# Loading the first feed-forward weights by rows of the contraction, zero matmuls ahead of them, one shared key block, and one filler moved

## The chip, the core and the metric

The kernel runs on one core of one Trainium2 chip. The metric is device time in microseconds (us) of one execution of the whole program. TensorE does the matmuls, ScalarE (ACT) and VectorE (DVE) the elementwise work, GpSimd (POOL) some of it, and SyncE (SP) issues most of the transfers from HBM.

## What is computed

The reference is two layers of an encoder for 320 tokens (256 of a prompt, 64 of a step with 256 cached ones), model width 1024. Cut to what matters here:

```python
for l in range(DEPTH):                                    # 2
    x = layer_norm(ALPHA * x + 0.5 * swiglu(x, f1_gu, f1_d), ...)      # 1024 -> 2 x 2816 -> 1024
    z = x @ w_in     # aq ak av  bq bk bv  iq ik iw  cq ck cv  gates
    bk = rope(bk, qpos)      # 64 columns: one key head for mixer B, returned too
    ik = rope(ik, qpos)      # 64 columns: one key head for B's indexer, returned too
    ...                      # mixers A (band), B (top-k by the indexer), C (differential), gated and merged
    x = layer_norm(ALPHA * x + merged @ w_out, ...)
    x = layer_norm(ALPHA * x + memory_attn(x, mem_k, mem_v, wm_q, wm_o), ...)
    x = layer_norm(ALPHA * x + 0.5 * swiglu(x, f2_gu, f2_d), ...)
```

The memory keys and values of the prompt (`mem_prompt @ w_mem_k`, `@ w_mem_v`) are computed for both layers as well.

## The kernel before, in words

Activations lie feature by token: a tile is 128 features by 320 tokens. Every fp32 value is kept as a pair, a rounded high part and the rest, so each product of a weight tile with an activation tile is three matmuls (`mm3`, L183 to L185: high by high, low by high, high by low). A weight block is 128 partitions by 1024 columns (512 KB); it holds the eight 128x128 tiles that one 128-wide output block contracts over. `prep` (L137 to L151) loads a block into a `raw` tile, ACT copies it to `hi` in two halves (L148) and DVE subtracts to get `lo` (L151). `raw`, `hi` and `lo` have three buffers each. `stream()` fixes the order of the blocks, and `ahead` and `nextw` keep two blocks ahead of the matmuls. A block is 24 matmuls of 320 columns.

The tile framework takes the program and decides the order on each engine by its own estimates; the queues are in order. Waits come from data, from buffers that are still read, and from PSUM: eight banks, four with the tag `mm` and four with the tag `at`.

**Start.** Before the first matmul the program loads one weight block in two halves and the input x (`load_x`, L202, and `split_x`, L205: cast, and subtraction on DVE and POOL). In the first feed-forward block (j = 0 of `ffn`, L485; L490 to L500) the gate product runs over all eight k's of x with the high part of the weights first, then with the low part; from then on every hidden block is a gate and an up product (48 matmuls in all) and an activation (L516 to L520).

**Mixers.** `attn_layer` (L531) projects values, then the index key `ik` and the four index queries (`QK0`), computes index scores and a top-k mask, and then runs the rest of the projections (`QK1`) in between the softmaxes of the three mixers. A mixer's turn is: scores (`scores`, L615, PE L625), softmax on DVE and ACT (`softmax`, L634 to L657), the transposition (`turn`, L660, PE L664 to L667), copies out of PSUM (for mixer C `c_turn`, L803, ACT L810 and DVE L811), the product with the values (`c_values`, L815, PE L817 to L822) with a root mean square on ACT (L828), POOL (L830, L831) and DVE (L834), and `c_finish` (L837). `projs(n)` (L848) puts n projections between these steps so that TensorE has work while the others finish. L667 writes a PSUM bank of the tag `at`, which the exponentials of the softmax last issued have to have read. `ik` and `bk` are both made by projecting the same 64 columns twice, so that the key lies on both halves of the partitions.

**Fillers.** The memory keys and values are 16 blocks for each layer, called fillers; they run inside the layer norms, where TensorE would wait. `FILL` (L62) says how many in each of the four norms of a layer. In a norm with n of them `before` (L1059, called after the fourth output block) runs n - 3, and `during` the last three while the statistics are formed. A filler's weights take a `raw` buffer too, and its `hi` and `lo` lie in tiles of the softmax.

Of the kernel before, what the change touches and what calls it, by code (L numbers as in the profile page):

```python
# [61 lines left out]
FILL = ((8, 8, 4, 4), (4, 4, 0, 0))  # L62
# [25 lines left out]
def ffn_stream(l, which):  # L88
    for j in range(FB):
# [8 lines left out]
def encoder(ctx: ExitStack, tc: tile.TileContext, a):  # L98
# [10 lines left out]
    def f(t):  # L109
        return t.bitcast(F32)  # L110
# [8 lines left out]
    def wtile(w=NT):  # L119
        return wk.tile([128, NT], F32, tag="w", bufs=8, name="w")[:, :w]  # L120
# [16 lines left out]
    def prep(src, cols, hi, lo, parts=1, hooks=None):  # L137
        raw = wp.tile([128, 1024], F32, tag="raw", name="raw")
        n = cols // parts
        for i in range(parts):  # L140
            c = slice(i * n, (i + 1) * n)
            if hooks:
                nc.sync.dma_start(raw[:, c], src[:, c])
            elif i == 0:
                nc.sync.dma_start(raw[:, :cols], src)
            if hooks:
                hooks[i][0]()
            act.activation(hi[:, c], raw[:, c], AF.Copy)  # L148
            if hooks:
                hooks[i][1]()  # L150
            dve.tensor_tensor(out=lo[:, c], in0=raw[:, c], in1=f(hi)[:, c], op=OP.subtract)  # L151
        return hi, lo
# [5 lines left out]
    def ahead(n, parts=2, hooks=None):  # L158
        while pos[0] < len(order) and len(ready) < n:
            key, cols = order[pos[0]]  # L160
            pos[0] += 1
            if key[0] == "wd":
                _, l, which, m, c0 = key
                src = a["wd"][l, which, m, :, c0 * 128:c0 * 128 + cols]
            else:
                src = a[key[0]]
                for i in key[1:]:
                    src = src[i]
            hi = wp.tile([128, 1024], F32R, tag="hi", name="hi")
            lo = wp.tile([128, 1024], F32R, tag="lo", name="lo")  # L170
            ready.append((key, prep(src, cols, hi, lo, parts, hooks)))
# [27 lines left out]
    x32 = one.tile([128, KB, NT], F32, name="x32")  # L199
# [11 lines left out]
    ahead(1, 2, ((lambda: (load_x(0), load_x(2)), lambda: split_x(0)),  # L211
                 (lambda: (load_x(4), load_x(6)), lambda: (split_x(2), split_x(4), split_x(6)))))
    ahead(2)
    x32 = [x32[:, m] for m in range(KB)]
# [269 lines left out]

    def ffn(l, which, x, norm):  # L485
        h = []
        for j in range(FB):
            pg, pu = psmm()[:, :NT], psmm()[:, :NT]
            wg = nextw("wgu", l, which, j, 0)
            if j == 0 and not (l or which):  # L490
                for k in range(KB):
                    c = slice(k * 128, (k + 1) * 128)
                    pe.matmul(pg, wg[0][:, c], x[k][0], start=(k == 0), stop=False)
                    pe.matmul(pg, wg[0][:, c], x[k][1], start=False, stop=False)
                for k in range(KB):
                    c = slice(k * 128, (k + 1) * 128)
                    pe.matmul(pg, wg[1][:, c], x[k][0], start=False, stop=(k == KB - 1))
                wu = nextw("wgu", l, which, j, 1)
                for k in range(KB):
                    mm3(pu, wu, x, k, k, k == 0, k == KB - 1)  # L500
            elif j == 0:
# [14 lines left out]
            s = wtile()  # L516
            act.activation(s, pg, AF.Silu)
            dve.tensor_tensor(out=s, in0=s, in1=pu, op=OP.mult)  # L518
            h.append(pair())
            split(s, h[j])  # L520
# [10 lines left out]
    def attn_layer(l, x, norm):  # L531
# [4 lines left out]
        kslot = {"ak": 0, "ck": 2, "bk": 6, "ik": 7}  # L536
        qk = {}
        SHUF = [(r + 8) % 16 if r < 16 else r for r in range(32)]

        def proj(name, i):  # L540
            p = block_mm(nextw("wqk", l, QK.index((name, i))), x)
# [12 lines left out]
            else:  # L554
                scaled = name in ("bq", "cq")
                sh, u = wtile(), wtile()
                dve.stream_shuffle(out=sh, in_=p, mask=SHUF)  # L557
                pool.tensor_tensor(out=sh, in0=sh, in1=sinS if scaled else sinT, op=OP.mult)  # L558
                dve.scalar_tensor_tensor(u, p, -0.125 if scaled else 1.0, cosT, op0=OP.mult, op1=OP.mult)
# [318 lines left out]
        projs(2)  # L878
# [347 lines left out]
```

## Time and profile before

| | |
|---|---|
| median of 3 runs | 1827.33 us (1826.3 to 1828.15) |
| the profiled execution: its own time | 1825.32 us |
| its span, first to last instruction | 1823.5 us |
| TensorE busy | 1770.3 us (97% of the span) |
| VectorE busy | 1158.6 us (64%) |
| ScalarE busy | 872.4 us (48%) |
| GpSimd busy | 274.1 us (15%) |
| mean granted TensorE clock | 0.991 of full speed |
| moved by DMA | 278.66 MB, 153 GB/s over the span |

The 1.8 us between the span and the execution's own time lie before the first and behind the last instruction. A row of the timeline gives the start in us from the span's start, the duration, engine and line of the kernel, operation, output and inputs by the program's names (without buffer numbers), partitions by columns, and in brackets how long the engine had been idle and whose end released it. A matmul's duration is longer than its distance to the next, since matmuls are pipelined: what one costs is read from the distance of two starts. "SPq" is a transfer being issued by SyncE. The granted clock is printed as a share of 2.4 GHz, so 0.5 is 1.2 GHz; up to the first record of a change, at 14.12 us, the view prints 1.00.

### The profile page before, as it was taken

Reading aid. Unit: us, or ns where it says so; the run is one execution under the profiler, and the core shown is the slowest. Engines: PE = TensorE matmul, PEld = TensorE weight load, DVE = VectorE, ACT = ScalarE, POOL = GpSimd, SP = SyncE. Lnnn points to the kernel's source line nnn. Section 1 sums busy time; section 2 is a strip of 40 time slices with the busy share of each in tenths; the row PEclk is TensorE's granted clock in tenths of the full one; section 3 lists DMA queues with packets and bytes.
Section 4 is the critical chain, followed back from the end, with each engine's and each line's share of the span. In section 5 each row is a group of like instructions: output and inputs, shape, how many; then the busy total and the mean of one; then the engine's idle time right before and its main releaser. Section 6 shows DMA issues by size and latency. Waiting matters only on the chain. (4 is left out here: it accounts for less than half of the span.)

```text
span 1823.5 us, 31668 instructions
## 1 busy us (share of the span) xinstructions
PE 1770.3 (97%) x12196; PEld 1718.2 (94%) x12196; DVE 1158.6 (64%) x2284; ACT 872.4 (48%) x1951; POOL 274.1 (15%) x297
## 2 busy tenths in 40 slices
PE   8999999989999999999999999999999999899997
PEld 8999999978998989999999999999889989899996
DVE  5544567986567785445564546679765786854455
ACT  5444435455455655444444444455554556444443
POOL 0000122230123040000210001222411220300012
PEclk9999999999999999999999999999999999999998
DMA  6544745434557544445544445454334572345442
GB/s 224 173 151 146 223 123 177 142 107 127 150 150 250 179 133 145 151 150 151 181 134 149 150 145 184 128 177 151 112 118 149 158 230 90 121 152 150 148 148 81
DMA packets 93176, 278.66 MB, mean 153 GB/s; under 512 B 12384, under 2 KB 26592, under 8 KB 92512
## 3 DMA queue, kind: packets, MB, share of 16 engines
q1 hardware_dynamic: 85536, 269.69, 48.1%
q10 hardware_dynamic: 7488, 6.95, 1.3%
q8 instruction: 95, 1.56, 0.3%
q14 instruction: 57, 0.47, 0.1%
HBM read 261.72 MB, written 14.88 MB: 152 GB/s over the span
## 5 line engine op out<-in xcount | busy, mean ns | idle before, releaser
L183 PE MATMUL mm<-slot,hi 128*128 128x320 f32 x3384 | 1054.5, 312 | 10.9 <-ACT slot L478 7.4
L185 PE MATMUL mm<-slot,hi 128*128 128x320 f32 x3384 | 1047.6, 310 | 1.7 <-DVE slot L480 1.6
L184 PE MATMUL mm<-slot,lo 128*128 128x320 f32 x3384 | 1048.5, 310 | 0.4 <-DVE lo L151 0.4
L151 DVE TENSOR_TENSOR lo<-raw,hi 128x512 fp32r<-128x512 f32 (+2 forms) x880 | 626.5, 750 | 362.3 <-ACT hi L148 359.4
L148 ACT ACTIVATE hi<-raw 128x512 fp32r<-128x512 f32 (+2 forms) x880 | 499.7, 614 | 579.8 <-issue 404.8
L183 PEld LDWEIGHTS mm<-slot,hi 128*128 128x128 f32 x3384 | 638.7, 189 | 18.9 <-ACT slot L478 8.9
L185 PEld LDWEIGHTS mm<-slot,hi 128*128 128x128 f32 x3384 | 637.4, 189 | 4.4 <-DVE slot L480 3.8
L184 PEld LDWEIGHTS mm<-slot,lo 128*128 128x128 f32 x3384 | 638.3, 189 | 1.1 <-DVE lo L151 0.8
L378 POOL TENSOR_TENSOR acc<-x 128x320 f32<-128x320 f32 x8 | 13.4, 1678 | 860.4 <-DVE x L407 681.8
L518 DVE TENSOR_TENSOR w<-w,mm 128x320 f32<-128x320 f32 x88 | 42.9, 488 | 132.1 <-PE mm L185 126.8
L378 POOL TENSOR_TENSOR acc<-acc,x 128x320 f32<-128x320 f32 x32 | 39.4, 1232 | 165.2 <-DVE x L407 165.2
L779 ACT ACTIVATE gate<-mm 128x320 f32<-128x320 f32 x48 | 21.0, 438 | 75.4 <-PE mm L185 75.4
L379 POOL TENSOR_TENSOR acc<-acc,w 128x320 f32<-128x320 f32 x40 | 49.9, 1247 | 39.6 <-ACT w L373 39.5
L558 POOL TENSOR_TENSOR w<-w,cst 128x320 f32<-128x320 f32 x32 | 28.1, 878 | 168.9 <-DVE w L557 119.2
L450 POOL TENSOR_TENSOR x<-x,msb 128x320 f32<-128x320 f32 x47 | 44.4, 977 | 50.7 <-ACT msb L436 50.7
L478 ACT ACTIVATE slot<-w,vec 128x320 fp32r<-128x320 f32 x56 | 33.9, 648 | 31.1 <-DVE w L467 31.1
L561 POOL TENSOR_TENSOR slot<-w 128x320 f32<-128x320 f32 (+2 forms) x44 | 42.8, 982 | 4.7 <-DVE st L654 2.3
L910 DVE SCALAR_TENSOR_TENSOR gate<-gate,mm 128x320 f32<-128x320 f32 x48 | 22.7, 483 | 32.5 <-PE mm L185 32.5
L197 DVE TENSOR_TENSOR slot<-w,slot 128x320 fp32r<-128x320 f32 x88 | 42.7, 485 | 0.5 <-ACT slot L196 0.5
L911 POOL TENSOR_TENSOR gate<-gate 128x320 f32<-128x320 f32 x16 | 14.1, 880 | 190.8 <-DVE gate L910 190.8
L373 ACT ACTIVATE w<-x 128x320 f32<-128x320 f32 x64 | 29.6, 462 | 25.3 <-DVE x L407 24.3
L649 ACT ACTIVATE e<-at,st 128x192 f32<-128x192 f32 (+4 forms) x60 | 24.3, 422 | 36.1 <-DVE st L643 36.1
(236 smaller groups left out, 1588.8 us busy)
## 6 DMA issues: line engine op xcount, KB each, us to landing
raw<-wgu SPq DMA_DIRECT2D x175, 512.0 KB, 3.5
raw<-wd SPq DMA_DIRECT2D x64, 512.0 KB, 3.6
raw<-wg SPq DMA_DIRECT2D x48, 512.0 KB, 3.6
raw<-wqk SPq DMA_DIRECT2D x40, 512.0 KB, 3.6
raw<-wd SPq DMA_DIRECT2D x32, 384.0 KB, 3.2
raw<-wmk SPq DMA_DIRECT2D x16, 512.0 KB, 3.7
raw<-wb SPq DMA_DIRECT2D x16, 512.0 KB, 3.6
raw<-wo SPq DMA_DIRECT2D x16, 512.0 KB, 3.7
```

The source lines that it names most:

```text
L148: act.activation(hi[:, c], raw[:, c], AF.Copy)
L151: dve.tensor_tensor(out=lo[:, c], in0=raw[:, c], in1=f(hi)[:, c], op=OP.subtract)
L183: pe.matmul(out, hi[:, c], x[kx][0], start=first, stop=False)
L184: pe.matmul(out, lo[:, c], x[kx][0], start=False, stop=False)
L185: pe.matmul(out, hi[:, c], x[kx][1], start=False, stop=last)
L197: (eng or dve).tensor_tensor(out=dst[1], in0=src, in1=f(dst[0]), op=OP.subtract)
L378: eng.tensor_tensor(out=self.acc1, in0=x32[0] if m == 1 else self.acc1, in1=x32[m], op=OP.add)
L379: pool.tensor_tensor(out=self.acc2, in0=self.sq0 if m == 1 else self.acc2, in1=sq, op=OP.add)
L450: eng.tensor_tensor(out=x32[m], in0=x32[m], in1=msb, op=OP.subtract)
L478: act.activation(x[m][0], u, AF.Identity, scale=g, bias=b)
L518: dve.tensor_tensor(out=s, in0=s, in1=pu, op=OP.mult)
L561: pool.tensor_tensor(out=d, in0=u[r, c], in1=sh[r, c], op=OP.add)
```

## The change

Four things, in the order of the program:

1. The first four hidden blocks of the first feed-forward (gate and up, eight outputs) are computed with the contraction outside: `ffn_first` takes for each k one weight block `wgs` (128 rows of the contraction by the 8 x 128 output columns), and accumulates into eight PSUM banks at once. x is loaded and split one k at a time, behind the weights of that k; the first one goes out on ACT's queue. The first weight block is loaded and split in four pieces, the second and third are loaded in two, and these loads and splits are kept in program order.
2. Eight matmuls of a zero tile, 512 columns each, stand ahead of the first real one.
3. `ik` and `bk` are one projection `kk`, each on one half of the partitions; the other half is filled by a transfer from SBUF to SBUF. One block of 24 matmuls less in each layer. The place in `QK1` that `bk` had is gone, and `projs(2)` between `c_turn` and `c_values` of C's second head is `projs(1)`.
4. `FILL` of layer 0 is (8, 8, 3, 5) and not (8, 8, 4, 4).

```diff
-QK0 = [("ik", 0)] + [("iq", i) for i in range(4)]
+QK0 = [("kk", 0)] + [("iq", i) for i in range(4)]
...
-       + [x for i in range(4) for x in (("cq", i), ("ck", i))] + [("bk", 0), ("bq", 0), ("bq", 1)])
+       + [x for i in range(4) for x in (("cq", i), ("ck", i))] + [("bq", 0), ("bq", 1)])
...
-FILL = ((8, 8, 4, 4), (4, 4, 0, 0))
+NJ0 = 4
+WARM = 8
+FILL = ((8, 8, 3, 5), (4, 4, 0, 0))
...
     def load_x(m):
-        nc.sync.dma_start(x32[:, m:m + 2], a["x"][:, m:m + 2])
+        (nc.sync if m else nc.scalar).dma_start(xin[:, m], a["x"][:, m])
 
     def split_x(m):
-        dve.tensor_copy(x[m][0], x32[:, m])
-        act.activation(x[m + 1][0], x32[:, m + 1], AF.Copy)
-        for i, eng in ((m, dve), (m + 1, pool)):
-            eng.tensor_tensor(out=x[i][1], in0=x32[:, i], in1=f(x[i][0]), op=OP.subtract)
+        tc.keep_in_program_order(dve.tensor_copy(x[m][0], xin[:, m]))
+        dve.tensor_tensor(out=x[m][1], in0=xin[:, m], in1=f(x[m][0]), op=OP.subtract)
...
+    load_x(0)
+    split_x(0)
+    ahead(1, 4, 4)
+    load_x(1)
+    split_x(1)
+    warm = one.tile([128, 512], BF, name="warm")
+    pool.memset(warm, 0.0)
+    wps = psat()
+    for i in range(WARM):
+        pe.matmul(wps, warm[:, 0:128], warm, start=True, stop=True)
...
+    def ffn_first(x, h):
+        pp = [(psmm()[:, :NT], psat()[:, :NT]) for _ in range(NJ0)]
+        for k in range(KB):
+            w = ready.pop(0)
+            hi, lo = w[1]
+            for j in range(NJ0):
+                for s in range(2):
+                    c = slice((j * 2 + s) * 128, (j * 2 + s + 1) * 128)
+                    pe.matmul(pp[j][s], hi[:, c], x[k][0], start=(k == 0), stop=False)
+                    pe.matmul(pp[j][s], lo[:, c], x[k][0], start=False, stop=False)
+                    pe.matmul(pp[j][s], hi[:, c], x[k][1], start=False, stop=(k == KB - 1))
+                if k == KB - 1:
+                    gated(*pp[j], h)
+            n = 2 if k == 0 else 1
+            ahead(1, 2, n)
+            if k + 2 < KB:
+                load_x(k + 2)
+                split_x(k + 2)
+            ahead(2, 2, n)
...
+        def proj_kk():
+            sh, u = rotated(block_mm(nextw("wqk", l, 0), x), False)
+            for n, b, r, other in (("ik", 7, slice(0, 64), slice(64, 128)), ("bk", 6, slice(64, 128), slice(0, 64))):
+                t = slot()
+                nc.scalar.dma_start(t[:, SEQ:SEQ + PAST], a["ck"][l, :, b])
+                for d, c in ((slice(0, SEQ), slice(0, SEQ)), (slice(SEQ + PAST, SEQ + PAST + STEP), slice(SEQ, NT))):
+                    pool.tensor_tensor(out=t[r, d], in0=u[r, c], in1=sh[r, c], op=OP.add)
+                    nc.sync.dma_start(t[other, d], t[r, d])
+                    nc.sync.dma_start(a["ok"][l, r, b, c], t[r, d])
+                qk[n, 0] = t
...
         p1 = c_turn(e1)
-        projs(2)
+        projs(1)
         w1 = c_values(1, *p1)
```

Where the order moves, three places.

**TensorE, the start of the program** (`warm` is the zero tile, `slot` a part of x, `mm` and `at` PSUM). Before:

```order
L493 MATMUL mm<-slot,hi 128x320
L494 MATMUL mm<-slot,hi 128x320
...
L497 MATMUL mm<-slot,lo 128x320 x8
L183 MATMUL mm<-slot,hi 128x320
L184 MATMUL mm<-slot,lo 128x320
```

Now:

```order
L224 LDWEIGHTS warm
L224 MATMUL at<-warm 128x512
...
L512 MATMUL mm<-slot,hi 128x320
L512 MATMUL at<-slot,hi 128x320
L512 MATMUL mm<-slot,hi 128x320
L513 MATMUL mm<-slot,lo 128x320
L514 MATMUL mm<-slot,hi 128x320
L513 MATMUL at<-slot,lo 128x320
```

Eight zero matmuls come first; then the eight outputs take turns on one k, where the old order went through all k's for one output.

**VectorE, mixer C's second turn in layer 0** (`pt<-at,w` is what `c_values` reads; the shuffle and the product with `cst` belong to a projection; the last row is C's normalisation). Before:

```order
L811 TENSOR_TENSOR pt<-at,w 128x256 x2
L811 TENSOR_TENSOR pt<-at,w 64x64
L151 TENSOR_TENSOR lo<-raw,hi 128x512
L557 STREAM_SHUFFLE w<-mm 128x320
L559 SCALAR_TENSOR_TENSOR w<-mm,cst 128x320
L151 TENSOR_TENSOR lo<-raw,hi 128x512 x2
L557 STREAM_SHUFFLE w<-mm 128x320
L559 SCALAR_TENSOR_TENSOR w<-mm,cst 128x320
L151 TENSOR_TENSOR lo<-raw,hi 128x512 x2
L834 TENSOR_SCALAR e<-e,st 128x128 x2
```

Now:

```order
L855 TENSOR_TENSOR pt<-at,w 128x256 x2
L855 TENSOR_TENSOR pt<-at,w 64x64
L154 TENSOR_TENSOR lo<-raw,hi 128x512
L570 STREAM_SHUFFLE w<-mm 128x320
L572 SCALAR_TENSOR_TENSOR w<-mm,cst 128x320
L154 TENSOR_TENSOR lo<-raw,hi 128x512 x2
L878 TENSOR_SCALAR e<-e,st 128x128 x2
```

One projection with its weights is gone between the turn and the normalisation.

**SyncE, the memory norm of layer 0** (`wmo` are the blocks of the output projection, `wmk` the fillers', `wgu` those of the next feed-forward). Before:

```order
L145 DMA raw<-wmo 128x1024
L145 DMA raw<-wmk 128x1024 x3
L301 DMA omk<-w 128x256
L302 DMA mkv_129<-w 128x256
L145 DMA raw<-wmo 128x1024 x2
L145 DMA raw<-wgu 128x1024 x6
```

Now:

```order
L149 DMA raw<-wmo 128x1024
L149 DMA raw<-wmk 128x1024 x2
L149 DMA raw<-wmo 128x1024 x2
L149 DMA raw<-wgu 128x1024 x6
```

One filler load less stands between the sixth `wmo` block and the last two.

## Rows read from the trace of the kernel before

**Rows 1.** Page of the profile, part 1: busy time, share of the span and instructions
```profile
PE 1770.3 (97%) x12196; PEld 1718.2 (94%) x12196; DVE 1158.6 (64%) x2284; ACT 872.4 (48%) x1951; POOL 274.1 (15%) x297
```

**Rows 2.** Page, part 5: line, engine, operation, shapes, count | busy us, mean ns | idle before
```profile
L183 PE MATMUL mm<-slot,hi 128*128 128x320 f32 x3384 | 1054.5, 312 | 10.9 <-ACT slot L478 7.4
...
L151 DVE TENSOR_TENSOR lo<-raw,hi 128x512 fp32r<-128x512 f32 (+2 forms) x880 | 626.5, 750 | 362.3 <-ACT hi L148 359.4
```

**Rows 3.** Timeline of the first 40 us: start us, us, engine, line, operation, tiles, shapes [idle before]
```profile
0.72 0.38 SPq L143 DMA_DIRECT2D raw<-wgu  x1
...
3.46 0.63 ACT L148 ACTIVATE hi<-raw 128x512 fp32r<-128x512 f32 x1 [1.47 <-DMA raw<-wgu]
...
4.42 0.33 DVE L206 CAST slot<-x 128x320 fp32r<-128x320 f32 x1 [3.02 <-DMA x<-x]
...
4.89 0.61 PE L493 MATMUL mm<-slot,hi 128*128 128x320 f32 x1 [4.89 <-ACT slot L207]
...
9.85 0.64 PE L494 MATMUL mm<-slot,hi 128*128 128x320 f32 x1 [0.39 <-DVE slot L209]
...
14.28 0.30 PE L183 MATMUL mm<-slot,hi 128*128 128x320 f32 x1
...
38.92 0.31 PE L183 MATMUL mm<-slot,hi 128*128 128x320 f32 x1
```

**Rows 4.** Busy time by stretch: us, engines' busy us (instructions), granted clock, DMA share, GB/s
```profile
4.89:14.28 9.39, 8.04 (x24) 6.36 (x25) 8.12 (x13) 5.62 (x9) 4.08 (x4) 1.00 0.99 333
...
659.40:669.70 10.30, 6.89 (x26) 6.35 (x25) 7.35 (x10) 4.69 (x9) 4.62 (x4) 0.67 0.81 236
1572.60:1577.50 4.90, 4.90 (x19) 4.90 (x19) 4.90 (x13) 2.66 (x5) 0.00 (x0) 0.51 0.00 0
```

**Rows 5.** Timeline of layer 0's mixers, 377 to 405 us: TensorE, VectorE, GpSimd
```profile
378.38 0.49 PE L817 MATMUL at<-slot,pt 128*128 128x128 f32 x2 [0.74 <-DVE pt L811]
...
387.58 0.39 PE L183 MATMUL mm<-slot,hi 128*128 128x320 f32 x1
...
394.70 0.38 PE L817 MATMUL at<-slot,pt 128*128 128x128 f32 x2
...
404.05 0.33 PE L667 MATMUL at<-cst,e 128*128 128x128 f32 x1 [1.35 <-ACT e L649]
...
391.53 1.00 DVE L811 TENSOR_TENSOR pt<-at,w 128x256 f32<-128x256 f32 x3
...
394.86 1.19 POOL L561 TENSOR_TENSOR slot<-w 128x320 f32<-128x320 f32 x1
...
399.95 0.87 POOL L831 TENSOR_TENSOR st<-st,mhalf 128x3 f32<-128x3 f32 x1
```

**Rows 6.** Timeline of layer 1's mixers, the same place: VectorE, TensorE
```profile
1301.35 1.00 DVE L811 TENSOR_TENSOR pt<-at,w 128x256 f32<-128x256 f32 x3
...
1306.07 0.38 PE L817 MATMUL at<-slot,pt 128*128 128x128 f32 x2
```

**Rows 7.** Timeline around layer 0's memory norm, 650 to 664 us: TensorE, VectorE, SyncE
```profile
650.11 0.28 PE L296 MATMUL mm<-big,e 128*128 128x256 f32 x1
...
652.27 0.28 PE L296 MATMUL mm<-big,e 128*128 128x256 f32 x1
...
662.59 0.61 PE L183 MATMUL mm<-slot,hi 128*128 128x320 f32 x1 [3.00 <-ACT hi L148]
663.61 0.64 PE L184 MATMUL mm<-slot,lo 128*128 128x320 f32 x1 [0.41 <-DVE lo L151]
...
652.41 2.66 DVE L151 TENSOR_TENSOR lo<-raw,hi 128x512 fp32r<-128x512 f32 x2
...
657.74 2.56 SPq L145 DMA_DIRECT2D raw<-wmo  x2
```

**Rows 8.** Timeline of layer 0's index keys: GpSimd, then TensorE's first scores
```profile
285.12 1.80 POOL L561 TENSOR_TENSOR slot<-w 128x256 f32<-128x256 f32 x2
...
298.21 0.66 PE L625 MATMUL at<-slot 64*64 64x320 f32 x6
```

More of the change, by code (lines that the diff above doesn't have):

```diff
@@ L88, in ffn_stream @@
 def ffn_stream(l, which):
-    for j in range(FB):
+    first = 0
+    if l == 0 and which == 0:
+        first = NJ0
+        for k in range(KB):
+            yield ("wgs", k), D
+    for j in range(first, FB):
         for s in range(2):
@@ L135, in stat, with prep @@
         return wk.tile([128, 8], F32, tag="st", bufs=8, name="st")
-    def prep(src, cols, hi, lo, parts=1, hooks=None):
+    def prep(src, cols, hi, lo, parts=1, pieces=1):
         raw = wp.tile([128, 1024], F32, tag="raw", name="raw")
+        n = cols // pieces
+        for i in range(pieces):
+            c = slice(i * n, (i + 1) * n)
+            nc.sync.dma_start(raw[:, c], src[:, c])
         n = cols // parts
@@ L141, in prep @@
             c = slice(i * n, (i + 1) * n)
[L142 to L151, printed above, removed]
+            a_i = act.activation(hi[:, c], raw[:, c], AF.Copy)
+            d_i = dve.tensor_tensor(out=lo[:, c], in0=raw[:, c], in1=f(hi)[:, c], op=OP.subtract)
+            if pieces > 1:
+                tc.keep_in_program_order(a_i)
+                tc.keep_in_program_order(d_i)
         return hi, lo
@@ L156, in encoder, with ahead @@
     pos = [0]
-    def ahead(n, parts=2, hooks=None):
+    def ahead(n, parts=2, pieces=1):
         while pos[0] < len(order) and len(ready) < n:
@@ L170, in ahead @@
             lo = wp.tile([128, 1024], F32R, tag="lo", name="lo")
-            ready.append((key, prep(src, cols, hi, lo, parts, hooks)))
+            ready.append((key, prep(src, cols, hi, lo, parts, pieces)))
     def nextw(*key):
@@ L483, in apply, with gated @@
             return x
+    def gated(pg, pu, h):
+        s = wtile()
+        act.activation(s, pg, AF.Silu)
+        dve.tensor_tensor(out=s, in0=s, in1=pu, op=OP.mult)
+        h.append(pair())
+        split(s, h[-1])
+    def ffn_first(x, h):
+        pp = [(psmm()[:, :NT], psat()[:, :NT]) for _ in range(NJ0)]
+        for k in range(KB):
+            w = ready.pop(0)
+            assert w[0] == ("wgs", k)
+            hi, lo = w[1]
[13 more added lines that the diff above has]
+            ahead(2, 2, n)
     def ffn(l, which, x, norm):
         h = []
-        for j in range(FB):
+        first = 0
+        if not (l or which):
+            ffn_first(x, h)
+            first = NJ0
+        for j in range(first, FB):
             pg, pu = psmm()[:, :NT], psmm()[:, :NT]
             wg = nextw("wgu", l, which, j, 0)
[L490 to L501, printed above, removed]
+            if j == 0:
                 wu = nextw("wgu", l, which, j, 1)
@@ L515, in ffn @@
                 load_mem()
[L516 to L520, printed above, removed]
+            gated(pg, pu, h)
         for m in range(KB):
@@ L534, in attn_layer, with rotated @@
         act.activation(toep, toep, AF.Copy, scale=-1.0)
[L536 removed]
+        kslot = {"ak": 0, "ck": 2}
         qk = {}
         SHUF = [(r + 8) % 16 if r < 16 else r for r in range(32)]
+        def rotated(p, scaled):
+            sh, u = wtile(), wtile()
+            dve.stream_shuffle(out=sh, in_=p, mask=SHUF)
+            pool.tensor_tensor(out=sh, in0=sh, in1=sinS if scaled else sinT, op=OP.mult)
+            dve.scalar_tensor_tensor(u, p, -0.125 if scaled else 1.0, cosT, op0=OP.mult, op1=OP.mult)
+            return sh, u
+        def proj_kk():
[8 more added lines that the diff above has]
+                qk[n, 0] = t
         def proj(name, i):
+            if name == "kk":
+                return proj_kk()
             p = block_mm(nextw("wqk", l, QK.index((name, i))), x)
@@ L554, in proj @@
             else:
[L555 to L559, printed above, removed]
+                sh, u = rotated(p, name in ("bq", "cq"))
                 for r, d, c in dst:
```

15 lines of the change are left out of this document (7 added, 8 removed).

## The prediction

> **What bounds the kernel now.** I read the page's busy times first: TensorE is busy for 97% of the span, VectorE for 64% [rows 1]. The costliest groups name the work: each of the three lines of a product has 3384 matmuls of 320 columns, 10152 in all, while the weights' splits on DVE stand idle for 362 us in total, waiting for their turn [rows 2]. A matmul's printed 312 ns is not its price, because neighbours overlap. The start-up rows give the price: the 25th matmul starts at 14.28 and the 193rd at 38.92, so 168 of them took 24.64 us, 0.147 us each [rows 3]. 10152 x 0.147 = 1489 us: the kernel is mostly a stream of matmuls at that pace, and a block of 24 costs 3.52 us wherever nothing else waits.
>
> So only two things count: matmuls removed, and stretches in which TensorE waits or runs at the lower of its two clock levels. The rows by stretch show that level: from 1572.6 to 1577.5 the granted clock is 0.51, 19 matmuls took 4.90 us, 0.26 each [rows 4], about what 1.2 GHz gives. The stretch 4.89 to 14.28 prints 1.00, but its 24 matmuls took 9.39 us [rows 4], 0.39 each, with waits in between: no clock record exists yet there, and I read it as the low level.
>
> **The start.** Before: 192 matmuls (four hidden blocks, gate and up, 24 each) are done when the 193rd starts, 38.92 [rows 3]. The first starts at 4.89, with half a weight block split at 3.46 and x cast at 4.42; the last wait for x ends at 9.85, and the clock is up by 14.28 [rows 3].
>
> Now the same 192 matmuls need only one k of x and a quarter of a block to begin.
> - Zero matmuls: no row shows one. 512/320 of 0.26 is 0.42 each, 3.3 us for eight; at the high level 0.235, 1.9 us. GpSimd must fill the tile first; I put their start at 1.2 us, so they end between 3.1 and 4.5. I take 4.5, since a program that has just begun is in the low level here.
> - First real data: the first weight load is issued at 0.72 and split from 3.46 [rows 3]; x's first part, 160 KB on ACT's queue, should be there by 3.5 to 4.2 and cast 0.33 later. First real matmul: 4.2 to 5.0, I take 4.6.
> - 192 x 0.147 = 28.2 us at the high level.
> - Cold part: before, TensorE ran without a wait from 9.85 and the clock was up at 14.28, 4.4 us later; at 1572.6 it took 4.9 us [rows 3, 4]. Counting the zero matmuls as work from 1.2, the rise comes between 5.6 and 6.5, say 6.2. The 1.6 us from 4.6 to 6.2 are then at half pace: 0.8 us lost.
> - End: 4.6 + 28.2 + 0.8 = 33.6, a gain of **5.3 us**. Bounds: 5.9 (rise at once), 3.7 (zeros not counted: rise at 9.5, 2.4 us lost).
>
> Supply: each k brings 512 KB of weights and 160 KB of x in 3.52 us, 195 GB/s; the start now moves 333 GB/s [rows 4]. The first two k's are 1.38 MB, and at the rates of the start they are in by some 6.1 us, split by 8.5, when TensorE asks for the second at 8.9. The activations of four hidden blocks come together at the end, but the next block's 3.52 us of matmuls need none of them: I count zero there.
>
> The first load in four pieces of 128 KB is the weak point, and the stretch's 333 GB/s was reached with loads of 256 to 512 KB [rows 4]. The Trainium skill (DMA: Bandwidth & Descriptors, section Bandwidth) speaks against such pieces: it asks for 1 MiB a transfer, with 341 GB/s at 1 MB and 138 at 64 KB. By that lower figure, as an estimate, the first k would be complete about 2 us later and the start would gain some 4 us.
>
> **One key block less.** 24 matmuls go in each layer, 3.52 us of TensorE, and with them one load, split and rotation that lie beside other work. But the block that goes was cover: in mixer C's second turn two blocks stood between transposition and values. In layer 0 they run from 387.58 to 394.70. With one, TensorE is through at 387.58 + 3.52 = 391.10 and then waits for the turned weights, which DVE finishes at 391.53 + 1.00 = 392.53 [rows 5]. The first turn shows this wait: 0.74 us for the same line at 378.38 [rows 5]. So the values start at 392.6, not 394.70: 2.1 us won, 1.4 waited.
>
> The wait is partly paid back. The next stall, at 404.05, is 1.35 us on the softmax's exponentials [rows 5], and they hang on C's normalisation: POOL's power at 399.95, which ended at 400.82 after the rotation of two queries. Now only one rotation stands there; its last step ends at 394.86 + 1.19 = 396.05 [rows 5], and ACT's squares end 2.1 earlier, near 395.8. POOL's three small steps (1.6 us) end at 397.7, 3.1 earlier, and the chain behind them moves with it: L667 near 401.0. TensorE arrives at 400.4. Gain in layer 0: **3.1 us**, between 2.1 (nothing paid back) and 3.5.
>
> Layer 1: DVE has the weights at 1301.35 + 1.00 = 1302.35 and the values start at 1306.07 [rows 6], with the clock at the low level for part of the two blocks. One block ends near 1302.5: 3.5 us won at the turn, then the same POOL chain bounds the rest. I take **3.1** again; bounds 2.1 and 3.5.
>
> The new key tiles: four additions for two (1.80 us more on GpSimd after 285.12) and four copies on SyncE's queue ahead of a weight load. The scores that read them start at 298.21 [rows 8]; the additions end about 288.7, so the copies have over 9 us. I price them at zero; without that cover each us would cost a us.
>
> **The filler.** In layer 0's memory norm TensorE waits 3.00 us at 662.59 and 0.41 at 663.61, then runs slow: granted 0.67 over 10.3 us [rows 7, 4], which costs 0.33 x 10.3 = 3.4 us. The late thing is the seventh `wmo` block: its load went out at 657.74, because its buffer was held by a filler. Moving one filler takes 24 matmuls of 256 columns away ahead of this wait; 18 steps from 650.11 to 652.27 are 0.12 each [rows 7], so 2.9 us of cover go too, and they come back in the next norm, which has no wait to fill. The load now follows the sixth block's split, which ends at 652.41 + 2.66 = 655.07 [rows 7]: 2.7 us earlier, and DVE has one filler split less (about 1.3) before it. So block seven starts about 3 us earlier, and 2.9 of that is only moved: some 0.1 left, with a wait as long as before. What can be won is the clock: between 0 and 3.4 us. I take **1.0**, near the lower end, because the wait stays; the lower bound is -1.
>
> **Sum.** 5.3 + 3.1 + 3.1 + 1.0 = 12.5 us. The profiled execution took 1825.32; 12.5 less is 1812.8. It stands 2.0 below the median of the three runs, 1827.33; from the median: **1814.8 us**.
>
> **Rivals.**
> - *The zero matmuls don't lift the clock, or the small first loads come late.* For: no row shows matmuls of zeros, or a 128 KB load at the start. Against: the low level ended each time after TensorE had been kept at work [rows 3, 4]. Price: 1.6 to 3 us of the start and, with the cover lost in the turns (2.1 each), a gain of 8: 1819. Chance 0.15.
> - *The filler's move ends the stall's slow clock altogether.* For: 3.4 us hang on it. Against: the wait keeps its length. Sum 5.3 + 6.2 + 4.5: 1811.3. Chance 0.12.
> - *Slower.* The copies of the key halves wait behind SyncE's other work and the index scores stand still. Price 1 us per us in both layers. It decides once they land after 298.2, and turns the sum when they land later than 298.2 + 12.5/2 = 304.4, some 17 us after issue; in the order they stand ahead of the next weight load. At 20 us: 1833. Chance 0.02.
> - *Nothing moves,* because the gains fall into other waits: TensorE is 97% busy [rows 1]. 1826, chance 0.02.
>
> The forecast has the remaining 0.69.
>
> **Range.** Low: 5.9 + 3.5 + 3.5 + 4 = 17 under the median, 1810.3; with the runs' own spread of a us, 1809.5. High: 3.7 + 2.1 + 2.1 - 1 = 6.9, 1820.4; 1820.5. 0.2% of this kernel is 3.7 us, about what a measurement can tell from no change: faster 0.95, within it 0.03, slower 0.02.
>
> **What would show it.** The 193rd product after the zeros, the fifth hidden block's first, starts near 33.6 instead of 38.92; the first real matmul near 4.6. C's second `c_values` starts with a wait of 1 to 1.5 us in layer 0, released by DVE's addition into `pt`, and L667 of the next turn comes with a wait under 1 us. In the memory norm a wait of 2 to 3 us remains before the seventh `wmo` block, and the granted clock behind it is again under 1.00. The forecast is wrong if TensorE waits between the k's of the first eight outputs, if `kk`'s copies release the first index scores, or if the next feed-forward norm of layer 0 shows a new wait.

## The result and the profile after

The changed kernel takes **1816.7 us** (median of 4 runs, 1815.87 to 1818.10) against 1826.82 for the kernel before in the same comparison: ratio **0.9944**, 95% interval 0.9927 to 0.9962, some 10 us faster. Run once more, it gave 0.9938 (0.9925 to 0.9950). The forecast was 1814.8, in a range of 1809.5 to 1820.5.

The profiled execution took 1818.1 us (span 1816.3), the slowest of its four, and that of before (1825.32) was faster than 34 of the 37 timed runs of before in all comparisons here. So the two profiles stand 7.2 us apart where the medians stand 10 apart. What follows is compared stage by stage.

The page of the profile after, part 1 (busy time, share, instructions) and the costliest line of part 5:

```profile
PE 1768.0 (97%) x12156; PEld 1713.7 (94%) x12156; DVE 1153.7 (64%) x2284; ACT 866.8 (48%) x1943; POOL 267.5 (15%) x292
...
L189 PE MATMUL mm<-slot,hi 128*128 128x320 f32 x3312 | 1033.2, 312 | 10.1 <-ACT slot L489 7.2
```

TensorE has 40 matmuls less: 48 of the two key blocks go, 8 zeros come. The share of 97% has not moved [rows 1].

**The start**, from the timeline of the first 40 us (start us, us, engine, line, operation):

```profile
1.30 3.60 PE L224 MATMUL at<-warm 128*128 128x512 bf16 x8 [1.30 <-POOL warm L221]
...
3.41 1.30 ACT L153 ACTIVATE hi<-raw 128x256 fp32r<-128x256 f32 x3 [0.96 <-DMA raw<-wgs]
...
4.33 0.83 PE L512 MATMUL mm<-slot,hi 128*128 128x320 f32 x1
...
4.96 0.47 PE L512 MATMUL at<-slot,hi 128*128 128x320 f32 x1
...
5.93 0.42 ACT L153 ACTIVATE hi<-raw 128x256 fp32r<-128x256 f32 x1 [1.22 <-DMA raw<-wgs]
...
7.34 0.31 PE L513 MATMUL at<-slot,lo 128*128 128x320 f32 x1
...
34.04 0.31 PE L189 MATMUL mm<-slot,hi 128*128 128x320 f32 x1
```

The eight zeros start 0.42 apart, the last at 4.26. The first real matmul is recorded from 4.33, but the second starts only 0.63 later, at 4.96, and the ones behind it 0.27 apart: so the zeros held TensorE until about 4.7. Ten real matmuls start before 7.34, at the low level, and the other 182 take 0.147 each up to the 193rd at 34.04, without a wait: 4.88 us earlier than before [rows 3].

**The turns of mixer C**, TensorE's timeline in layer 0, then in layer 1:

```profile
382.59 0.34 PE L711 MATMUL at<-cst,e 128*128 128x128 f32 x1 [1.90 <-ACT e L693]
...
387.81 0.38 PE L861 MATMUL at<-slot,pt 128*128 128x128 f32 x2
...
395.93 0.33 PE L711 MATMUL at<-cst,e 128*128 128x128 f32 x1 [0.17 <-ACT e L693]
```

```profile
1290.77 0.33 PE L711 MATMUL at<-cst,e 128*128 128x128 f32 x1 [1.37 <-ACT e L693]
...
1295.89 0.49 PE L861 MATMUL at<-slot,pt 128*128 128x128 f32 x2 [1.27 <-DVE pt L855]
...
1304.12 0.33 PE L711 MATMUL at<-cst,e 128*128 128x128 f32 x1 [0.19 <-ACT e L693]
...
1313.97 0.66 PE L710 MATMUL at<-cst,e 128*128 128x128 f32 x4 [1.72 <-DVE slot L888]
```

Layer 1 shows the forecast pattern: a wait of 1.27 on the turned weights, then 0.19 in the third turn where there were 1.35 in layer 0 before [rows 5]. (In layer 1 before, that wait was missing: the level was low from 1297.5 to 1300.9.) In layer 0 the wait at 387.81 is missing because the one block ran at the low clock level (382.8 to 386.2). In the second profile of the changed kernel the level is up there, and the forecast wait, 1.26 at 387.75, stands in its place; with layer 1's it makes up this row of that profile's waits (us in total, times, longest):

```profile
PE at L861 <- DVE pt L855: 2.5, 2, 1.3
```

The last row above, L710 in layer 1, will matter. Before, the same wait (then L666) was 1.44:

```profile
1323.43 0.66 PE L666 MATMUL at<-cst,e 128*128 128x128 f32 x4 [1.44 <-DVE slot L844]
```

**The memory norm of layer 0**, TensorE, VectorE and SyncE:

```profile
652.92 0.41 PE L189 MATMUL mm<-slot,hi 128*128 128x320 f32 x1 [2.15 <-ACT hi L153]
655.18 0.41 PE L190 MATMUL mm<-slot,lo 128*128 128x320 f32 x1 [1.84 <-DVE lo L154]
...
645.71 2.65 DVE L154 TENSOR_TENSOR lo<-raw,hi 128x512 fp32r<-128x512 f32 x2
...
651.31 1.48 DVE L154 TENSOR_TENSOR e<-raw,e 128x1024 fp32r<-128x1024 f32 x1
652.71 1.15 DVE L395 SCALAR_TENSOR_TENSOR x<-x,csb 128x320 f32<-128x320 f32 x1
653.78 1.94 DVE L154 TENSOR_TENSOR lo<-raw,hi 128x512 fp32r<-128x512 f32 x2
...
648.39 2.95 SPq L149 DMA_DIRECT2D raw<-wmo  x2
```

The load goes out right behind the sixth block's split (645.71 + 2.65 = 648.36), as worked out. But TensorE now waits twice: 2.15 for the high part, 1.84 for the low part, 3.99 in all where it was 3.41 [rows 7]. The low part comes late because a filler's split (1.48) and a shift (1.15) stand ahead of it on VectorE.

Busy time by stretch (us, PE PEld DVE ACT POOL, granted clock, DMA share, GB/s), layer 1's last turn and the memory norm:

```profile
1309.00:1314.60 5.60, 3.88 (x42) 2.71 (x41) 3.28 (x11) 2.64 (x12) 1.11 (x3) 1.00 0.61 189
1314.60:1318.00 3.40, 3.40 (x15) 3.36 (x14) 2.03 (x8) 2.62 (x12) 0.20 (x1) 0.50 0.00 0
650.40:655.80 5.40, 1.41 (x8) 0.92 (x7) 5.40 (x7) 2.77 (x5) 4.17 (x3) 1.00 0.75 229
655.80:659.30 3.50, 3.50 (x15) 3.50 (x14) 3.50 (x5) 1.62 (x3) 2.47 (x2) 0.51 0.64 210
```

Right behind the wait at 1313.97, and behind that at 655.18, the level is the low one (0.50 and 0.51, so 1.2 of 2.4 GHz) for some 3.4 us. Before, the level was low for 6.8 us behind the memory norm's wait (662.7 to 669.5), and not at all in layer 1's last turn.

### The profile page after: what moved, and what is told of

It is laid out like the page before. It is cut to its first block, busy times and chain, and to the rows that moved or that the text cites. A ratio compares the mean times of both kernels' runs of the same rounds, so it can differ in the third digit from the quotient of the medians.

```text
span 1816.3 us, 31596 instructions
## 1 busy us (share of the span) xinstructions
PE 1768.0 (97%) x12156; PEld 1713.7 (94%) x12156; DVE 1153.7 (64%) x2284; ACT 866.8 (48%) x1943; POOL 267.5 (15%) x292
## 5 line engine op out<-in xcount | busy, mean ns | idle before, releaser
L189 PE MATMUL mm<-slot,hi 128*128 128x320 f32 x3312 | 1033.2, 312 | 10.1 <-ACT slot L489 7.2
L190 PE MATMUL mm<-slot,lo 128*128 128x320 f32 x3312 | 1027.1, 310 | 1.9 <-DVE lo L154 1.8
L191 PE MATMUL mm<-slot,hi 128*128 128x320 f32 x3312 | 1026.2, 311 | 1.7 <-DVE slot L491 1.6
L154 DVE TENSOR_TENSOR lo<-raw,hi 128x512 fp32r<-128x512 f32 (+3 forms) x878 | 622.0, 747 | 360.8 <-ACT hi L153 358.1
L153 ACT ACTIVATE hi<-raw 128x512 fp32r<-128x512 f32 (+3 forms) x878 | 498.1, 613 | 580.1 <-issue 392.9
L189 PEld LDWEIGHTS mm<-slot,hi 128*128 128x128 f32 x3312 | 626.0, 189 | 18.9 <-ACT slot L489 9.1
L191 PEld LDWEIGHTS mm<-slot,hi 128*128 128x128 f32 x3312 | 624.6, 189 | 4.4 <-DVE slot L491 3.8
L190 PEld LDWEIGHTS mm<-slot,lo 128*128 128x128 f32 x3312 | 625.4, 189 | 2.8 <-DVE lo L154 2.4
L418 DVE TENSOR_TENSOR x<-x,mm 128x320 f32<-128x320 f32 x56 | 27.0, 482 | 21.3 <-PE mm L191 21.3
```

What stands on the lines that cost most here:

```text
L153: a_i = act.activation(hi[:, c], raw[:, c], AF.Copy)
L154: d_i = dve.tensor_tensor(out=lo[:, c], in0=raw[:, c], in1=f(hi)[:, c], op=OP.subtract)
L189: pe.matmul(out, hi[:, c], x[kx][0], start=first, stop=False)
L190: pe.matmul(out, lo[:, c], x[kx][0], start=False, stop=False)
L191: pe.matmul(out, hi[:, c], x[kx][1], start=False, stop=last)
```

## Where the time went, stage by stage, in all runs

The table gives how much each stage grew (+) or shrank (-) in us against the profile of before. A stage runs from one matmul to another that both kernels have, and its length is the difference of their starts in the timelines. The stages: *start*, to the 193rd matmul (38.92 before); *keys 0* and *keys 1*, from the first turn of mixer A's values (348.65, 1258.54) to L667 of C's third turn (404.05, 1313.87); *last turn 1*, from there to 1336.46; *memory norm 0*, from 640.65 to 929.95, so that a moved filler is counted in; *between*, from 425.59 to 640.65; *tail*, from 1336.46 to 1810.03.

```
                 start  keys 0  between  memory   keys 1  last     tail
                                         norm 0           turn 1
after            -4.88  -3.24    1.38     0.10    -3.13    1.84     1.12
again            -5.22  -2.85    0.05     0.08    -3.15    1.85     0.98
start_alone      -5.01   0.02    0.04    -1.07     0.39    0.03    -0.45
keys_alone        0.27  -3.19    1.07    -1.07    -3.15    1.86     0.77
filler_alone      0.70  -0.02    0.30    -0.03    -0.38    0.01     0.18
no_zeros         -3.38  -3.19    0.37     0.06    -2.77    0.29     1.84
fill_back        -5.40  -3.21    0.24    -2.11    -3.18    0.00     1.25
zeros_ffn        -5.49  -3.21    0.16     0.05    -3.13    1.87     0.85
zeros_turn       -5.11  -3.22    0.22     0.08    -3.14    1.10     1.45
back_late        -5.16  -3.21    0.04    -1.00    -3.14    0.02     1.89
move_late        -5.34  -3.22   -0.02     0.03    -3.16    0.29     0.40
back_raw4        -5.05  -3.21    2.17    -4.26    -3.15    0.02     0.15
one_piece        -3.58  -3.23    0.19     1.41    -3.18    0.28    -0.10
```

Most stages in which nothing was edited repeat to 0.1 us from run to run. *Between* and *tail* scatter by 1 to 2, and a stage moves by up to 1.3 with the clock level in it: in `one_piece` and `move_late` the level was low for 6.8 us in the memory norm, in the others, but for `back_raw4`, for 3.4. The start of before came out 0.3 and 0.7 longer in two other profiles of it (`keys_alone`, `filler_alone`), so the gains of the start are at the low end. Times are compared with the kernel before, run beside each group of four.

## The experiments

### The same kernel, and each part alone

`again` is the changed kernel, unedited.

> The changed kernel once more, nothing edited. In its first profile, TensorE ran at the lower clock level in the mixers at 345.2, 382.8, 1277.1 and 1314.6, and behind the memory norm's wait at 655.8. Theory: where the level falls is chance from one execution to the next, and the first profile (1818.1) was one with much of it. Then the time stays near 1816.7, and the new profile shows the low stretches in other places or another number of them, with the waits before the same instructions as before. Rival: the places are set by the order of the work; then the same five come back within a us.

Measured: 1815.83, ratio 0.9938 (0.9925 to 0.9950). Half of each. In layer 0's mixers the low stretches moved (one from 367.8 to 374.6 in place of two at 345 and 383), but the three at 654.5, 1275.7 and 1313.3 came back behind the same waits. So in part the order of the work sets them: they are not all chance.

`start_alone` is the changed kernel without the key block and with the filler moved back. Its edit against the changed kernel (a part; `proj_kk` goes too):

```diff
-QK0 = [("kk", 0)] + [("iq", i) for i in range(4)]
+QK0 = [("ik", 0)] + [("iq", i) for i in range(4)]
...
-FILL = ((8, 8, 3, 5), (4, 4, 0, 0))
+FILL = ((8, 8, 4, 4), (4, 4, 0, 0))
...
-        projs(1)
+        projs(2)
```

> The kernel before with the new start alone (loads by contraction, the first four hidden blocks with k outside, zero matmuls); keys and fillers as before. Theory: the parts add up, and the start is worth the 4.9 us by which the 193rd matmul came earlier in the changed kernel (34.04 for 38.92): 1821.9. Rival: of these 4.9 a part is eaten by the waits of the norms behind it, which hang on other engines: 1823.5 or more.

Measured: 1819.5, ratio 0.9958 (0.9946 to 0.9971), 8.1 below its 1827.59. The stage itself gives 5.01, and nothing behind it eats that, so the rival falls. The profile has 1.07 more in the memory norm, where the level was low for 3.4 us and not 6.8 as in the profile of before. What is left of the 8 lies within the interval (2.4 us either way).

`keys_alone` is the kernel before with `kk`, `proj_kk` and `projs(1)` alone.

> The kernel before with one shared key block alone (and one block less of cover in the second turn). Theory: 3.1 us in each layer as forecast, 1820.6; the changed kernel's profile showed 3.2 in layer 0 and 1.3 in layer 1, where stretches at the lower clock took the rest, by chance. Rival: layer 1 loses it each time, because the missing cover leaves a wait, and behind a wait the clock falls: about 1822.3.

Measured: 1821.72, ratio 0.9965 (0.9952 to 0.9979), 5.9 less. The time lies between the two theories; the stages decide. The keys give 3.19 and 3.15 up to the third turn, as forecast, and layer 1 loses 1.86 in the last turn each time so far. But the wait behind which it loses it is not the one that was missing cover: it is L710's on `c_finish` (1.72, as above), 0.28 longer than in the three profiles without the key block.

`filler_alone` is the kernel before with this line alone:

```diff
-FILL = ((8, 8, 4, 4), (4, 4, 0, 0))
+FILL = ((8, 8, 3, 5), (4, 4, 0, 0))
```

> The kernel before with the filler's move alone. In the changed kernel's profile the wait ahead of the seventh block of the memory norm became 2.1 us before the first matmul and 1.8 before the second (3.0 and 0.4 before), and the low stretch half as long. Theory: within a us of the kernel before, 1826.8, since the load is won 2.7 us and the cover of 2.9 us is lost. Rival: the clock behind it stays up and 3 us are won, 1823.8. Slower by 1 to 2 us if the next norm now waits.

Measured: 1827.19 (11 runs), ratio 0.9999 (0.9991 to 1.0008). No gain, as the theory has it; the clock rival falls.

### Zero matmuls: at the start, and in two waits

`no_zeros`:

```diff
-WARM = 8
+WARM = 0
```

> The changed kernel without its eight zero matmuls. Theory: they count as work for the clock. Without them TensorE begins at about 4.3, the level rises some 4.4 to 4.9 us later, near 9, in place of 6.0 to 7.3, and two to three more us run at half pace: the 193rd matmul starts near 35.1 in place of 33.7 to 34.0, the time is 1.1 to 1.4 us longer, 1817.3. Rival: zeros do nothing for the clock; then the rise and the 193rd matmul stay where they were, and the time too.

Measured: 1818.55, ratio 0.9955 (0.9942 to 0.9967). By the time alone this can't be told from the changed kernel, since the intervals overlap; the start's rows decide:

```profile
4.07 0.61 PE L512 MATMUL mm<-slot,hi 128*128 128x320 f32 x1 [4.07 <-DVE slot L212]
...
10.34 0.43 PE L512 MATMUL at<-slot,hi 128*128 128x320 f32 x1
10.60 0.31 PE L513 MATMUL at<-slot,lo 128*128 128x320 f32 x1
...
35.54 0.31 PE L189 MATMUL mm<-slot,hi 128*128 128x320 f32 x1
```

The first real matmul comes earlier, at 4.07, but the steps stay at 0.27 until 10.60, and the 193rd starts at 35.54: 1.5 us later than in the changed kernel, 1.85 than in `again`. Zeros lift the clock; the rival falls. The rise came 1.6 us later than the theory had it (near 9): 6.5 us behind the first matmul, with one wait of 0.16 at 4.83.

`zeros_ffn` (`warm` is the zero tile of the start; `pg` takes a whole PSUM bank here):

```diff
+    def zeros(p, n):
+        for _ in range(n):
+            pe.matmul(p, warm[:, 0:128], warm, start=True, stop=True)
...
+            if j == 0 and l == DEPTH - 1 and which:
+                zeros(pg, 30)
```

> The changed kernel with 30 zero matmuls of 512 columns between the last statistics of layer 1's memory norm and the feed-forward block behind them, where TensorE waits 5.8 us and ran at the lower level for some 5 us afterwards in both profiles of the changed kernel (to 1570.6 and 1569.3). Theory: zeros keep the level up, the wait itself stays as long, and half of those 5 us is won: 2.4 us, near 1814. Rival: the level falls all the same, the zeros then take twice as long and end behind the wait: no gain, or a loss of up to 5 us.

Measured: 1816.36, ratio 0.9947 (0.9934 to 0.9961): no gain. The same stretch of `zeros_ffn`, then of `again`:

```profile
1558.60:1570.00 11.40, 10.17 (x54) 6.65 (x53) 10.93 (x26) 4.01 (x7) 4.66 (x5) 1.00 0.13 45
```

```profile
1558.40:1569.30 10.90, 5.51 (x21) 5.01 (x20) 10.46 (x24) 3.77 (x7) 4.80 (x6) 0.69 0.15 50
```

and TensorE's timeline in `zeros_ffn` from the last 23 zeros on (the other seven fell between the statistics):

```profile
1558.67 5.13 PE L229 MATMUL mm<-warm 128*128 128x512 bf16 x23
1563.45 0.50 PE L189 MATMUL mm<-slot,hi 128*128 128x320 f32 x1
...
1564.78 0.42 PE L191 MATMUL mm<-slot,hi 128*128 128x320 f32 x1 [0.68 <-DVE slot L496]
...
1567.10 0.41 PE L191 MATMUL mm<-slot,hi 128*128 128x320 f32 x1 [0.27 <-DVE slot L496]
```

The level stays up (1.00 for 0.69), as the theory said, and yet nothing is won: at full pace TensorE waits for the low parts of the normalised x, which VectorE, busy for 10.93 of 11.40 us, hands out. The low level cost nothing there, because VectorE bounds that stretch. Both theories had left this out.

`zeros_turn`: seven zeros, by the same helper, in `turn` ahead of the second group of transposes, for C's last head alone.

```diff
+            if warmed:
+                zeros(psmm(), warmed)
             for i, c in enumerate((EOF[2] + 128, EOF[3] + 128, EOF[4], EOF[4] + 128)):
...
-        p3 = c_turn(e3)
+        p3 = c_turn(e3, 7)
```

> The changed kernel with seven zero matmuls in each layer between the two groups of transposes of mixer C's last turn, where TensorE waits 1.72 us in layer 0 and 1.99 in layer 1; behind the latter the level fell in all three profiles with the shared key block (1314.6, 1313.3, 1317.7), and never in the other three, where that wait is 1.71. Theory: this low stretch is what layer 1 lost of the keys' gain (3.2 us at the third turn, 1.3 behind it); with zeros it does not come, and 1.6 us are won: 1814.6. Rival: the level falls anyway, since the low stretch follows an earlier one (1277) and not this wait: 1816.3, as the changed kernel.

Measured: 1817.52, ratio 0.9950 (0.9937 to 0.9962). The level does not fall in layer 1's last turn, and the stage loses 1.10 in place of 1.85. But layer 0 loses 1.24 where it had lost nothing: the zeros changed the order, so that nine matmuls of the gate block no longer stand between the last two groups of transposes, and a wait on the turned weights shows in their place. The clock part of the theory holds, and the edit is no gain.

### The filler moved back, and the late load

`fill_back`:

```diff
-FILL = ((8, 8, 3, 5), (4, 4, 0, 0))
+FILL = ((8, 8, 4, 4), (4, 4, 0, 0))
```

> The changed kernel with the filler moved back to the memory norm. From that norm to the end of the next one, the runs with the move won 0.0 us on the profile of before (the changed kernel twice, the filler alone), those without it 1.1 us (the start alone, the keys alone), where the level fell once behind the wait and not twice. Theory: the move itself gives nothing and may cost 1.1, so this is 1 us faster than the changed kernel, 1815. Rival: no difference, because the old order loses as much again when the level falls twice, as in the profile of before; or 1 us slower, as the prediction had it.

Measured: **1813.18** (1812.48 to 1814.79), ratio 0.9929 (0.9916 to 0.9941). The intervals against the kernel before overlap with the changed kernel's; but `zeros_ffn` and `zeros_turn`, which were timed beside it, have the filler where the change put it and no gain of their own, took 1815.11 to 1819.08, and so `fill_back` is some 3 us faster, by more than expected. Rows of `fill_back` (TensorE in the memory norm; L710's waits of both layers, us in total, times, longest; then layer 1's last turn by stretch):

```profile
653.65 0.63 PE L189 MATMUL mm<-slot,hi 128*128 128x320 f32 x1 [2.43 <-ACT hi L153]
```

```profile
PE at L710 <- DVE slot L888: 2.9, 2, 1.4
```

```profile
1309.00:1318.00 9.00, 8.23 (x71) 7.16 (x72) 5.62 (x18) 5.85 (x25) 1.03 (x3) 1.00 0.25 76
```

One wait of 2.43 in place of 2.15 and 1.84, the stage 2.2 us shorter (in `start_alone` and `keys_alone`, which have four fillers too, 1.2 shorter, with waits of 3.6 in all); and in layer 1's last turn the level stays up (1.00), 1.84 us more. That second gain was not expected. The longest wait of L710 is 1.4 us in the six profiles that lose nothing there (that of before among them) and 1.7 in seven others (`zeros_turn` has its own): in four of the seven the level falls behind it and 1.85 are lost, in three it does not and 0.28 are lost. The 0.28 arises on ScalarE, which starts its squares (L872) that much later and waits for nothing that the profile shows. Why was not settled: it goes with neither the filler's place nor the key block alone, since `filler_alone` has 1.44 with the filler moved, and `keys_alone` has 1.72 with the filler where it was.

`back_late` issues the fillers' loads one block later in the memory norm, with the filler moved back; `move_late` does the same with the filler where the change put it.

```diff
+            self.at = KB // 2 if li % 4 == 2 else KB // 2 - 1
...
-            if m == KB // 2 - 1 and self.before:
+            if m == self.at and self.before:
```

> The changed kernel with the filler moved back (four in layer 0's memory norm) and, in the memory norm alone, the fillers' loads issued one block later, behind the load of the seventh block of the product. Theory: TensorE waits there 2.7 to 3.4 us because that load stands behind three filler loads and needs a raw buffer that a filler holds; one block later every load has 3.5 us more, the wait goes and the level does not fall behind it: 3 to 4.5 us less than with the filler moved back alone (1813.2), 1809 to 1810. Rival: the splits on VectorE are the bottleneck, not the loads' order; then the wait only moves to the eighth block, with the same length: 1813.

Measured: 1814.36, ratio 0.9930 (0.9918 to 0.9942). The theory falls: the wait is at the eighth block, 3.2 us in all (2.88 and 0.32; 3.4 before), because that block's load now stands behind the fillers (TensorE, then SyncE):

```profile
658.13 0.41 PE L189 MATMUL mm<-slot,hi 128*128 128x320 f32 x1 [2.88 <-ACT hi L153]
```

```profile
652.80 0.33 SPq L149 DMA_DIRECT2D raw<-wmo  x1
```

> The changed kernel as it is (three fillers in that norm) with the fillers' loads one block later in the same way. Theory: the wait of 3.9 us goes here too, and with it the whole difference between three and four fillers: 3 to 4.5 us less than the changed kernel, 1812 to 1813, and 1810 if layer 1's low stretch behind the last turn stays away as it did with the filler moved back. Rival: the wait moves to the eighth block: 1816.

Measured: 1813.25, ratio 0.9927 (0.9914 to 0.9939). Its memory norm gives 0.03. Here too the wait moved to the eighth block, where TensorE waits 1.75 for the high part (654.20) and 1.05 for the low part (655.66). It is 1.2 us shorter (2.80 for 3.99), but the level is low for 6.8 us behind it and not for 3.4. That the kernel is some 3 us below the changed one comes from elsewhere: layer 1's last turn loses 0.29 in place of 1.84, and *between* loses nothing, where the first profile of the changed kernel lost 1.38.

`back_raw4`, the filler moved back and four buffers for raw weights:

```diff
-        raw = wp.tile([128, 1024], F32, tag="raw", name="raw")
+        raw = wp.tile([128, 1024], F32, tag="raw", bufs=4, name="raw")
...
-NSLOT = 30
+NSLOT = 28
```

> The changed kernel with the filler moved back and a fourth raw buffer, for which two of the thirty slots go. Theory of the late load: the seventh block's load is issued a buffer earlier and the wait of 2.7 us is gone or under 1 us; 2 to 4 us less than 1813.2, unless the two slots that are missing make another wait. Rival (splits on VectorE): the wait stays, 1813.

Measured: **1812.43**, ratio 0.9923 (0.9909 to 0.9936), the fastest here, though not to be told from `fill_back`. Its memory norm, the load of the last two blocks (issued at 649.37 in `fill_back`), TensorE's row and the stretches:

```profile
646.06 3.96 SPq L149 DMA_DIRECT2D raw<-wmo  x2
...
655.18 0.41 PE L190 MATMUL mm<-slot,lo 128*128 128x320 f32 x1 [0.71 <-DVE lo L154]
```

```profile
650.00:655.20 5.20, 4.49 (x32) 4.22 (x30) 5.20 (x7) 3.88 (x7) 2.83 (x2) 1.00 0.77 237
655.20:659.00 3.80, 3.80 (x26) 3.80 (x27) 3.80 (x6) 2.04 (x5) 2.73 (x3) 1.00 0.83 285
```

The load goes out 3.3 us earlier, the wait for it is gone, 0.71 us are left on VectorE's split, the level stays up, and the stage is 4.26 us shorter than before, 2.15 shorter than in `fill_back`. So the buffer makes the wait, as the theory had it, and the order of the loads alone only moves it. Some 2 us go again in *between*: TensorE waits 1.00 at 526.64 (0.17 in `fill_back`) and 0.64 at 577.54 (0.31), and from 580.4 the level is low for 3.4 us, as in no other profile. That the two missing slots make these waits was not tried apart.

### The first load in one piece

`one_piece`:

```diff
-    ahead(1, 4, 4)
+    ahead(1, 4, 1)
```

> The changed kernel with its first weight block loaded in one transfer of 512 KB in place of four of 128 KB. In the changed kernel the first of the four was split at 3.41 and TensorE began at 4.33, never waiting for the others. Theory: one transfer lands later as a whole (the median is 3.5 us from issue to landing), near 4.2, and TensorE begins at about 5.0, so 0.5 to 0.7 us are lost: 1817. Rival (small transfers cost rate): the whole block is there earlier than now, and the time is the same or up to 1 us better.

Measured: 1817.36, ratio 0.9946 (0.9932 to 0.9960), by the time alone the same as the changed kernel. The rows of its start:

```profile
1.62 0.91 SPq L149 DMA_DIRECT2D raw<-wgs  x2
...
4.77 2.75 ACT L153 ACTIVATE hi<-raw 128x256 fp32r<-128x256 f32 x6 [2.33 <-DMA raw<-wgs]
...
4.99 0.33 DVE L212 CAST slot<-x 128x320 fp32r<-128x320 f32 x1 [3.58 <-DMA x<-x]
...
5.47 0.61 PE L512 MATMUL mm<-slot,hi 128*128 128x320 f32 x1 [0.58 <-DVE slot L212]
```

The first split comes 1.36 later than with four pieces, and the first part of x, issued at 0.71 in both, is cast at 4.99 in place of 3.60; the 193rd matmul comes 1.3 us later. As a whole the block is there earlier with one transfer: all of it is split from 4.77 on without a wait, where the last of the four pieces is split at 5.93. But TensorE begins with the first piece, and none of the others made it wait. The loads of the next blocks now leave at 1.62 (3.05 with four pieces); that the first data share the way with them fits this, and was not tried apart. The rival is right on the block and wrong on the start.

## Why the prediction was right, and where not

- **The start: right.** Forecast 5.3 with an end at 33.6; measured 4.88, 5.22 and 5.01, ends at 34.04, 33.69 and 33.91. The zeros held TensorE until about 4.7, where 4.5 was taken for their end and 4.6 for the first real matmul, so they and not the data set that start. The level was up at 7.3 in the first profile and 6.0 in the second for a forecast of 6.2; in the first, ten matmuls at 0.27 lost 1.2 us for the 0.8 of the forecast, which is the 0.4 that is missing. The supply was as tight as worked out: in the two profiles in which the level rose at 5.1, TensorE waited 0.1 to 0.2 for the low part of the second k. The pieces that were called the weak point are a strong one: TensorE never waits for them, and one transfer of 512 KB costs 1.3 us more. By the figures of the Trainium skill (DMA: Bandwidth & Descriptors, section Bandwidth: 138 GB/s at 64 KB, 341 at 1 MB, measured there on loads that GpSimd issues) the prediction put the first k, as an estimate, about 2 us later and the gain at some 4. The traces agree on the block, which is complete later in pieces (split at 5.93, for 4.77 in one transfer), and not on the gain, 4.9 to 5.5 in nine profiles.
- **The keys in layer 0: right**, 3.24 for 3.1 (2.85 in `again`), paid back in the third turn as worked out: L711 comes at 395.93 with 0.17 us of wait. The copies of the key halves hold nothing up, as priced: from the 193rd matmul to 348.65, with the index scores in between, the length is that of before to 0.02 us in both profiles of the changed kernel.
- **The keys in layer 1: right as far as it was worked out, and lost behind it.** 3.13 were won at the third turn, for 3.1. The step that failed is that the working ends there, with "then the same POOL chain bounds the rest", and keeps the whole gain: one turn further TensorE's wait grew by 0.28 and the level fell behind it, together 1.84 us. Net 1.3, below the bound of 2.1. The prediction weighed the clock at the start and in the memory norm, and not behind the turns.
- **The filler: wrong sign.** Forecast 1.0 gained; the stage gives 0.1 lost, and with four fillers 1.1 won (`start_alone`, `keys_alone`) to 2.1 (`fill_back`). The load came 2.6 us earlier, as worked out (2.7). The step that failed is the wait "as long as before": only the wait for the high part was priced. The low part was now late too, because with the load earlier VectorE still had a filler's split and a shift ahead of it (1.84 for 0.41). And the 3.4 us that hung on the clock were those of one execution, whose level was low for 6.8 us; every other profile with four fillers in that norm and three raw buffers was at the low level for 3.4 us. The next norm shows no new wait, as taken.
- **The sum.** 12.5 was worked out from the profiled execution; the two profiled executions of the changed kernel stand 7.2 and 8.7 below it, since 1.8 (layer 1), 1.1 (the filler), 0.1 to 0.4 (the start) and 1 to 2.5 us in *between* and *tail*, not traced further, are missing. The medians stand 10.1 to 11.8 apart, because the profiled execution of before was a fast one. So that 1814.8 came this near is in part luck: its terms promised 4 to 5 us more than the profiles gave, and the start point of the sum hid more than half of it.
- **Slips in the working.** With the rise at once the start's bound is 6.1 and not 5.9 (4.6 + 28.2). The 4 and 4.5 us for the filler, in the range and the rival, exceed what the rows give, 3.4 and 0.1. And before, TensorE was not without a wait from 9.85: its weight loads waited for x again at 10.77 and 11.29, 0.15 and 0.24.

## What to carry to other kernels

A wait on the critical path has two prices, its length and what TensorE loses at the lower clock level behind it. The second was paid in layer 1's last turn, where TensorE bounds the work that follows, and not in `zeros_ffn`'s stretch, where VectorE does; so look at the other engines' busy time there before filling a wait with zero matmuls. Where a load is late for want of a buffer, changing the order of the loads only moved the wait here, and a fourth buffer took it away. A stage that ends in a gain can lose it in the next one: follow the chain one stage past the edit.

## What was not expected of the hardware

- Eight zero matmuls of 512 columns in bf16, from 1.3 us on, brought the rise of the level from 10.6 (one profile, `no_zeros`) to between 5.1 and 7.3 (nine profiles with the start as changed).
- Small loads at the start were the better ones: four of 128 KB took SyncE 1.81 us to issue and kept the later loads back by 1.4 us, and the first data came 1.4 us earlier than with one of 512 KB, though the last came 1.2 us later.
- A wait that was 0.28 us longer went, in part of the profiles, with 1.6 us more: behind 1.7 us of L710 in layer 1 the level fell in four profiles of seven, both of the changed kernel among them, and behind 1.4 in none of six.
